# Sums of squares and two-element copies taken off GpSimd, and another beginning, in a two-layer hybrid decoder

## The chip, the cores and the metric

The kernel runs on one core of one Trainium2 chip. The metric is the device time of one execution in microseconds, as a median over several executions. The engines are named as the profile names them: PE is TensorE, PEld its weight load, DVE is VectorE, ACT is ScalarE, POOL is GpSimd, SP is SyncE, which issues the DMAs here.

## The reference

Two decoder layers run over x (256 positions, width 1024), all in float32. A vector c conditions every norm through a scale, a shift and a gate per feature:

```python
def rmsnorm(x, g):
    y = xf * lax.rsqrt(jnp.mean(xf * xf, axis=-1, keepdims=True) + RMS_EPS)
    return (y * g).astype(x.dtype)
def modulate(h, shift, scale):
    return h * (1 + scale[:, None, :]) + shift[:, None, :]

cs = jax.nn.silu(c)
mod = cs @ mod_w[l] + mod_b[l]                   # six vectors of 1024: sh_m, sc_m, g_m, sh_f, sc_f, g_f
h = modulate(rmsnorm(x, norm_mix[l]), sh_m, sc_m)
mix = rglru_mixer(...) if l == 0 else moba_mixer(...)
x = x + g_m[:, None, :] * mix
h = modulate(rmsnorm(x, norm_ffn[l]), sh_f, sc_f)
x = x + g_f[:, None, :] * swiglu(h, w_gate, w_up, w_down)
```

Before layer 1, x is normed once more for a shared key/value projection with its own shift and scale. The output is a last rmsnorm of x. The mixer of layer 0 is a gated linear recurrence with input and output projections; that of layer 1 is causal attention with 8 heads on 4 key/value heads. The feed-forward width is 2816.

## The kernel before, in words

**Layout.** Features lie on the partitions, positions on the free axis: x is eight tiles of 128x256, one for each group k of 128 features. A norm therefore sums over partitions. `sumsq` (lines 521 to 552) does it: ACT squares the eight tiles (L529), the squares are added up to fewer tiles (L538), and a product with a 128x128 matrix of ones (L543, "ones product" below, two PE instructions in float32) leaves the sum on every partition. ACT takes the root (L546), DVE the reciprocal (L551). The adds of the first norm, n0, run on DVE; those of the three later ones, f0, n2 and f1, run on POOL, six each, after which two tiles are left (`"sqpe": 1`) and two ones products follow.

**Products.** A float32 weight is split into a high part (ACT, L438) and a low part (DVE, L439), and one product is three fast matmuls (`mm3`, L386 to L388): high by high, high weight by low operand, low weight by high operand. A few products run in plain float32 instead (L448, L675), two PE instructions each.

**Borders.** In front of the products that follow a norm, the kernel does not wait for the norm. `unnorm` (lines 584 to 601) multiplies x by its scale alone, and the reciprocal root is applied to the product's result. The shift travels along as two more columns of the same operand: the tiles are 128x258. These columns are written by copies of two elements a partition on POOL, for the plain operand (L588) and for the high and low operand (L595). The names: `f_u` is the operand and `f_g` the product at the start of each feed-forward block (f0 in layer 0, plain, f1 in layer 1, split), `f_p` the products behind it; `kv_u` and `kp` are operand and product of the key projection (border n2); `f_d` is the down product of the feed-forward, `ao` the output product of the attention, `wo` that of the recurrence. The residuals that make the new x are on L609. L599 makes the low operand on DVE, L597 the high one on ACT.

**Scales and shifts.** A column of a modulation vector comes from a 512 KB block of weights in a slot of the pool `mraw` (three slots), which DVE multiplies by csb, the row silu(c) on all partitions, and sums up (L461); `_m` names are such vectors. Others go over PE.

**Start.** SP loads the row c (4 KB) into one partition of an `mraw` slot, then x, the small vectors and the first blocks. PE spreads the row with two ones products (L421), ACT takes Silu from PSUM (L423). Then the first norm, and for each k a column of scale and shift, the normed tile (L556), its high and low part (L562, L566, L567) and the input projection `xb` and `yb` (L675 and split).

**What sets the order.** A planner, `Plan` (lines 93 to 265), records every operation with a modelled cost, its buffers and a rank, which is its place in the program plus an offset from a table `PRIO` (by engine and name), and lists the operations per engine; each engine then runs its list in that order, and waits where an operand is missing. `KN` holds further offsets. The planner decides on every engine, SP's list of DMAs included.

## Time and profile before

| | |
|---|---|
| three runs | 622.88, 622.90, 624.37 us (median 622.90) |
| the profiled execution | 623.06 us |
| its span in the trace | 621.2 us |
| mean granted TensorE clock | 0.991 |
| TensorE busy | 593.1 us, 95% of the span, 4688 instructions |
| VectorE busy | 471.9 us, 76% |
| ScalarE busy | 338.1 us, 54% |
| GpSimd busy | 34.9 us, 6%, 68 instructions |
| moved by DMA | 162.95 MB, 262 GB/s in the mean |

The profiled execution took 623.06 us, of which 621.2 lie in the span of the trace; 1.9 us are outside it. In the order of time the stages are: the start and the input projection (to 52 us), the recurrence (52 to 107), its output product (to 135), border f0 and the first feed-forward (135 to 331), border n2 with the key projection (331 to 349), attention (349 to 419), border f1 and the second feed-forward (419 to 613), and a last norm. In the timeline a row is start, duration, engine, line, operation and tiles, count; a bracket gives the idle time before it and what released it. A matmul row lasts longer than the step to the next one, since they are pipelined.

### The profile page before, as it was taken

What the parts mean: (1) busy time and instruction counts of PE and PEld (TensorE: products, weight loads), DVE (VectorE), ACT (ScalarE), POOL (GpSimd) and SP (SyncE); (2) the same over time, 40 slices, a digit from 0 to 9 for tenths busy, and PEclk for the clock granted to TensorE, in tenths of its full rate; (3) what the DMA queues carried; (4) which work ended last, traced back from release to release, by engine and by line L of the source; (5) the groups of instructions that cost most, each with busy time, mean ns of one, the idle gap of its engine ahead of it and who ended that gap; (6) DMA issues with size and microseconds to landing.
All of it is one profiled execution on the core that took longest, in us unless ns stands there. A gap on an engine that the chain in (4) does not pass through costs nothing.

```text
span 621.2 us, 11500 instructions
## 1 busy us (share of the span) xinstructions
PE 593.1 (95%) x4688; PEld 569.8 (92%) x4688; DVE 471.9 (76%) x718; ACT 338.1 (54%) x485; POOL 34.9 (6%) x68
## 2 busy tenths in 40 slices
PE   3999999988999999999997999998999999999996
PEld 1899878987999999999996999997999999999996
DVE  6998888887988898998755799997997555545542
ACT  5537998537654344342445988766555434333322
POOL 0000000032000000001006000016000000000000
PEclk9999999999999999999998999997999999999999
DMA  8896897687988899898888257885696553445501
GB/s 297 335 356 241 326 390 324 244 316 293 413 314 313 326 332 329 331 342 345 325 314 286 70 203 306 301 323 190 213 333 234 181 179 141 140 143 187 185 1 69
DMA packets 33363, 162.95 MB, mean 262 GB/s; under 512 B 3700, under 2 KB 4893, under 8 KB 23966
## 3 DMA queue, kind: packets, MB, share of 16 engines
q1 hardware_dynamic: 33310, 162.21, 70.5%
q8 instruction: 37, 0.61, 0.4%
q14 instruction: 16, 0.13, 0.1%
...
## 4 chain that ended last, share of the span: by engine, by line
PE 80%; ACT 6%; DVE 4%; DMA 4%; POOL 2%; issue 2%; SPq 0%; DVEq 0%; POOLq 0%; ACTq 0%
PE ps_f_p L388 12%; PE ps_f_p L386 12%; PE ps_f_p L387 12%; PE ps_f_d L388 6%; PE ps_f_d L386 6%; PE ps_f_d L387 6%; PE ps_xb L675 2%; PE ps_f_g L448 2%; PE ps_yb L386 1%; PE ps_yb L388 1%; PE ps_yb L387 1%; PE ps_qp L388 1%; PE ps_qp L386 1%; PE ps_qp L387 1%; DMA mraw_mr_sc_f_m__1482<-in_mod 1%
## 5 line engine op out<-in xcount | busy, mean ns | idle before, releaser
L386 PE MATMUL ps_f_p<-t_f_h,whi_f0b_h 128*128 128x256 f32 x320 | 89.8, 281 | 0.0
L388 PE MATMUL ps_f_p<-t_f_h,wlo_f1b_l 128*128 128x256 f32 x320 | 89.6, 280 | 0.0
L387 PE MATMUL ps_f_p<-t_f_l,whi_f0b_h 128*128 128x256 f32 x320 | 89.4, 279 | 0.0
L388 PE MATMUL ps_f_p<-t_f_h,wlo_f0b_l 128*128 128x256 f32 x320 | 89.3, 279 | 0.0
L386 PE MATMUL ps_f_p<-t_f_h,whi_f1b_h 128*128 128x256 f32 x320 | 89.3, 279 | 0.0
L387 PE MATMUL ps_f_p<-t_f_l,whi_f1b_h 128*128 128x256 f32 x320 | 89.3, 279 | 0.0
L439 DVE TENSOR_TENSOR wlo_f1b_l<-raw_f1b_r,whi_f1b_h 128x2048 fp32r<-128x2048 f32 x20 | 45.8, 2289 | 21.0 <-ACT whi_f1b_h L438 20.9
L387 PEld LDWEIGHTS ps_f_p<-t_f_l,whi_f1b_h 128*128 128x128 f32 x320 | 60.2, 188 | 0.0
L388 PEld LDWEIGHTS ps_f_p<-t_f_h,wlo_f0b_l 128*128 128x128 f32 x320 | 60.2, 188 | 0.0
L386 PEld LDWEIGHTS ps_f_p<-t_f_h,whi_f0b_h 128*128 128x128 f32 x320 | 60.1, 188 | 0.0
L388 PEld LDWEIGHTS ps_f_p<-t_f_h,wlo_f1b_l 128*128 128x128 f32 x320 | 60.1, 188 | 0.0
L387 PEld LDWEIGHTS ps_f_p<-t_f_l,whi_f0b_h 128*128 128x128 f32 x320 | 59.9, 187 | 0.1
L386 PEld LDWEIGHTS ps_f_p<-t_f_h,whi_f1b_h 128*128 128x128 f32 x320 | 59.8, 187 | 0.0
L438 ACT ACTIVATE whi_f1b_h<-raw_f1b_r 128x2048 fp32r<-128x2048 f32 x20 | 38.1, 1911 | 26.5 <-issue 19.1
L439 DVE TENSOR_TENSOR wlo_f0b_l<-raw_f0b_r,whi_f0b_h 128x2048 fp32r<-128x2048 f32 x20 | 45.7, 2289 | 8.3 <-ACT whi_f0b_h L438 8.3
L438 ACT ACTIVATE whi_f0b_h<-raw_f0b_r 128x2048 fp32r<-128x2048 f32 x20 | 38.1, 1910 | 21.7 <-issue 18.5
L386 PE MATMUL ps_f_d<-t_f_ah,whi_f0c_h 128*128 128x256 f32 x176 | 49.4, 281 | 0.0
L388 PE MATMUL ps_f_d<-t_f_ah,wlo_f1c_l 128*128 128x256 f32 x176 | 49.3, 280 | 0.0
L388 PE MATMUL ps_f_d<-t_f_ah,wlo_f0c_l 128*128 128x256 f32 x176 | 49.1, 279 | 0.0
L386 PE MATMUL ps_f_d<-t_f_ah,whi_f1c_h 128*128 128x256 f32 x176 | 49.1, 279 | 0.0
L387 PE MATMUL ps_f_d<-t_f_al,whi_f1c_h 128*128 128x256 f32 x176 | 49.1, 279 | 0.0
L387 PE MATMUL ps_f_d<-t_f_al,whi_f0c_h 128*128 128x256 f32 x176 | 49.1, 279 | 0.0
...
## 6 DMA issues: line engine op xcount, KB each, us to landing
...
```

The costliest lines, as they stand in the source:

```text
L386: nc.tensor.matmul(o, h_, a_, start=start, stop=False, skip_group_check=skip)
L387: nc.tensor.matmul(o, h_, b_, start=False, stop=False, skip_group_check=skip)
L388: nc.tensor.matmul(o, l_, a_, start=False, stop=stop, skip_group_check=skip)
L438: act(n - o, lambda: nc.scalar.activation(hi.ap[:, o:n], raw.ap[:, o:n], AF.Copy), (raw,), (hi,))
L439: tt(n - o, lambda: nc.vector.tensor_sub(lo.ap[:, o:n], raw.ap[:, o:n], hi.f[:, o:n]), (raw, hi), (lo,))
L448: pe(n * 0.0016875 + 0.002, lambda: nc.tensor.matmul(ps.ap[:, c:c + n], lo.ap[:, o:o + w], xh.ap[:, xo:xo + n], start=start, stop=stop, sk ...
L675: pe(0.432, lambda k=k, m=m, c=c, ps=ps, wr=wr, f=f: nc.tensor.matmul(ps.ap[:, c:c + S], wr.ap[:, m * P:(m + 1) * P], f.ap[:, :S], start=( ...
```

## The change

1. **Another beginning.** The row c is no longer loaded into one partition. One DMA writes it to all 128 partitions of csb at once (512 KB written from a 4 KB row); it is fifth in SP's list, behind the four of x. One ACT Silu over 128x1024 follows in place. The two products on L421, the two Silus on L423 and the use of an `mraw` slot are gone.
2. **First norm.** The seven DVE adds of n0 become eight ones products: every square goes to PE.
3. **Norms at the borders.** For f0, n2 and f1 the six POOL adds become three DVE adds (of the first four squares), and five ones products instead of two (`"sqpe": 4`).
4. **Two-element copies.** Those of the high and of the plain operand go to ACT, those of the low operand to DVE: 8 on ACT in f0, 8 on ACT and 8 on DVE in n2 and in f1.
5. **The table of offsets** `PRIO` is another one on all engines, so the order moves everywhere, and POOL keeps 15 instructions.

```diff
-    "shat": 0, "gmat": 1, "win": 600, "tol": 3.6321997149340305e-16, "nn": 5, "nyh": 1, "sqpe": 1, "gnat": 5,
+    "shat": 0, "gmat": 1, "win": 600, "tol": 3.6321997149340305e-16, "nn": 5, "nyh": 1, "sqpe": 4, "gnat": 5,
...
     "PE": {
-        "cps": -707, "xb": 191, "ga": -492, "sh_f_ps": -94, "sh_f_pt": 1070, "wo": 33, "g_m_ps": 4, "g_m_pt": -155,
+        "n_st": 2072, "xb": -905, "yb": 4848, "ga": 540, "sh_f_ps": 1082, "sh_f_pt": -11, "wo": 288, "g_m_ps": -779,
...
-        crow = pl.buf("mraw", "crow")
-        load(crow, 8, lambda: crow.ap[0:1, :], t["c_row"])
+        pl.op("SP", 0.6, lambda: nc.sync.dma_start(csb.ap, t["c_row"].to_broadcast([P, D])), (), (csb,), lat=1.0)
...
-        silu = []
-        for i in range(2):
-            cps = PS(f"cps{i}")
-            c = slice(i * 512, (i + 1) * 512)
-            pe(0.86, lambda cps=cps, c=c: nc.tensor.matmul(cps.ap, ones.ap[0:1, :], crow.ap[0:1, c], start=True,
-                                                           stop=True), (ones, crow), (cps,))
-            silu.append(act(512, lambda cps=cps, c=c: nc.scalar.activation(csb.ap[:, c], cps.ap, AF.Silu), (cps,),
-                            ((csb, i),), AF.Silu))
+        silu = [act(D, lambda: nc.scalar.activation(csb.ap, csb.ap, AF.Silu), (csb,), (csb,), AF.Silu)]
...
-        def sumsq(xs, name, on_dve=False, prev=(), then=None):
+        def sumsq(xs, name, on_dve=False, on_pe=False, prev=(), then=None):
...
-                if acc is None:
+                if acc is None or on_pe:
                     acc = sq
                     parts.append(acc)
-                elif on_dve or k < KC - KN["sqpe"]:
+                elif (on_dve and name == "n0") or k < KC - KN["sqpe"]:
...
-                gp(2, 0.003, lambda: nc.gpsimd.tensor_copy(f.ap[:, S:], sh.ap[:, k:k + 1].to_broadcast([P, 2])), (sh,),
-                   ((f, 1),))
+                act(2, lambda: nc.scalar.activation(f.ap[:, S:], sh.ap[:, k:k + 1].to_broadcast([P, 2]), AF.Copy), (sh,),
+                    ((f, 1),))
...
-            for d, s_ in ((hi, shc[0]), (lo, shc[1])):
-                gp(2, 0.003, lambda d=d, s_=s_: nc.gpsimd.tensor_copy(d.r[:, S:], s_.r[:, k:k + 1].to_broadcast([P, 2])),
-                   (s_,), ((d, 1),))
+            act(2, lambda: nc.scalar.activation(hi.r[:, S:], shc[0].r[:, k:k + 1].to_broadcast([P, 2]), AF.Copy),
+                (shc[0],), ((hi, 1),))
+            tt(2, lambda: nc.vector.tensor_copy(lo.r[:, S:], shc[1].r[:, k:k + 1].to_broadcast([P, 2])), (shc[1],),
+               ((lo, 1),))
...
-        rstd0 = sumsq(x0, "n0", on_dve=True)
+        rstd0 = sumsq(x0, "n0", on_pe=True)
...
-            rstd = sumsq(xs, name, prev=(gelus, exps)[l], then=AF.Silu)
+            rstd = sumsq(xs, name, True, prev=(gelus, exps)[l], then=AF.Silu)
...
-        rstd2 = sumsq(x2, "n2", prev=silus[0], then=AF.Exp)
+        rstd2 = sumsq(x2, "n2", True, prev=silus[0], then=AF.Exp)
```

The lines of the changed kernel are six or seven lower than those of the kernel before: its splits are on L431 and L432, its square adds on L531, its residuals on L603, its low operands on L593 and its two-element copies on L587 (ACT) and L589 (DVE).

**Border n2 on DVE.** In the order of before, from the split of the value weights to the first low operands (`t_f0x` are the new x tiles, `ps_f_d` the down product, `t_kv_u_l` the low operand of the key product):

```order
L439 TENSOR_TENSOR wlo_wv_l<-raw_wv_r,whi_wv_h 128x2048
L609 SCALAR_TENSOR_TENSOR t_f0x_3748<-ps_f_d_3656,g_f_m,t_x_7_1573 128x256
L599 SCALAR_TENSOR_TENSOR t_kv_u_l<-t_f0x_3241,sc_kv_m,t_kv_u_h 128x256
L439 TENSOR_TENSOR wlo_wv_l<-raw_wv_r,whi_wv_h 128x2048
L599 SCALAR_TENSOR_TENSOR t_kv_u_l<-t_f0x_3319,sc_kv_m,t_kv_u_h 128x256
L599 SCALAR_TENSOR_TENSOR t_kv_u_l<-t_f0x_3416,sc_kv_m,t_kv_u_h 128x256
L599 SCALAR_TENSOR_TENSOR t_kv_u_l<-t_f0x_3494,sc_kv_m,t_kv_u_h 128x256
```

And in the changed kernel:

```order
L432 TENSOR_TENSOR wlo_wv_l<-raw_wv_r,whi_wv_h 128x2048
L593 SCALAR_TENSOR_TENSOR t_kv_u_l<-t_f0x_3229,sc_kv_m,t_kv_u_h 128x256
L593 SCALAR_TENSOR_TENSOR t_kv_u_l<-t_f0x_3313,sc_kv_m,t_kv_u_h 128x256
L603 SCALAR_TENSOR_TENSOR t_f0x_3759<-ps_f_d_3649,g_f_m,t_x_7_1574 128x256
L531 TENSOR_TENSOR t_n_sq_3761<-t_n_sq_3761,t_n_sq_3763 128x256
L531 TENSOR_TENSOR t_n_sq_3761<-t_n_sq_3761,t_n_sq_3765 128x256
L531 TENSOR_TENSOR t_n_sq_3761<-t_n_sq_3761,t_n_sq_3767 128x256
L432 TENSOR_TENSOR wlo_wv_l<-raw_wv_r,whi_wv_h 128x2048
L589 COPY t_kv_u_l<-kv_sl 128x2
L593 SCALAR_TENSOR_TENSOR t_kv_u_l<-t_f0x_3392,sc_kv_m,t_kv_u_h 128x256
```

The three square adds come onto DVE's list between the last residual and the second split of the value weights, and each low operand from the fourth on has a two-element copy ahead of it. The low operands of k = 1 and 2 now stand ahead of the last residual, with their copies earlier in the list.

**Border f1 on DVE.** In the order of before, from the shift vector to the third low operand (`ps_ao` is the attention's output product, `t_x` the new x, `wlo_f1a` the low part of the weights of `f_g`):

```order
L512 TENSOR_TENSOR sh_f_m<-sh_f_m,vec 128x8
L599 SCALAR_TENSOR_TENSOR t_f_u_l<-t_x_0_4798,sc_f_m,t_f_u_h 128x256
L609 SCALAR_TENSOR_TENSOR t_x_4_4839<-ps_ao_4572,g_m_m,t_f0x_3494 128x256
L609 SCALAR_TENSOR_TENSOR t_x_5_4851<-ps_ao_4572,g_m_m,t_f0x_3579 128x256
L581 TENSOR_TENSOR f_sl<-sh_f_m,f_sh 128x8
L439 TENSOR_TENSOR wlo_f1a_l<-raw_f1a_r,whi_f1a_h 128x2048
L599 SCALAR_TENSOR_TENSOR t_f_u_l<-t_x_1_4803,sc_f_m,t_f_u_h 128x256
L609 SCALAR_TENSOR_TENSOR t_x_6_4891<-ps_ao_4597,g_m_m,t_f0x_3668 128x256
L609 SCALAR_TENSOR_TENSOR t_x_7_4896<-ps_ao_4597,g_m_m,t_f0x_3748 128x256
L439 TENSOR_TENSOR wlo_f1b_l<-raw_f1b_r,whi_f1b_h 128x2048
L599 SCALAR_TENSOR_TENSOR t_f_u_l<-t_x_2_4815,sc_f_m,t_f_u_h 128x256
```

And in the changed kernel:

```order
L505 TENSOR_TENSOR sh_f_m<-sh_f_m,vec 128x8
L531 TENSOR_TENSOR t_f_sq_4804<-t_f_sq_4804,t_f_sq_4816 128x256
L603 SCALAR_TENSOR_TENSOR t_x_4_4832<-ps_ao_4559,g_m_m,t_f0x_3490 128x256
L531 TENSOR_TENSOR t_f_sq_4804<-t_f_sq_4804,t_f_sq_4823 128x256
L574 TENSOR_TENSOR f_sl<-sh_f_m,f_sh 128x8
L603 SCALAR_TENSOR_TENSOR t_x_5_4850<-ps_ao_4559,g_m_m,t_f0x_3581 128x256
L531 TENSOR_TENSOR t_f_sq_4804<-t_f_sq_4804,t_f_sq_4830 128x256
L603 SCALAR_TENSOR_TENSOR t_x_6_4859<-ps_ao_4576,g_m_m,t_f0x_3661 128x256
L589 COPY t_f_u_l<-f_sl 128x2
L593 SCALAR_TENSOR_TENSOR t_f_u_l<-t_x_0_4792,sc_f_m,t_f_u_h 128x256
L589 COPY t_f_u_l<-f_sl 128x2
L593 SCALAR_TENSOR_TENSOR t_f_u_l<-t_x_1_4799,sc_f_m,t_f_u_h 128x256
```

The split of `wlo_f1a` that stood ahead of the second low operand now stands behind it (it follows the residual of k = 7), and the three adds are interleaved with the residuals of k = 4 to 6.

**The start on DVE.** In the order of before, from the last adds of the first norm to the first normed tile (`mraw_mr_sc` and `mraw_mr_sh` are the blocks of the first scale and shift column):

```order
L641 TENSOR_SCALAR sp_m<-sp_neg 128x10
L538 TENSOR_TENSOR t_n_sq_218<-t_n_sq_218,t_n_sq_244 128x256
L461 SCALAR_TENSOR_TENSOR mraw_mr_sc__236,sc_138<-mraw_mr_sc__236,csb 128x1024
L661 SCALAR_TENSOR_TENSOR sc_138<-sc_138,b_137,vec 128x1
L461 SCALAR_TENSOR_TENSOR mraw_mr_sh__250,sh_139<-mraw_mr_sh__250,csb 128x1024
L551 RECIPROCAL t_n_rstd<-t_n_rstd 128x256
L664 TENSOR_TENSOR sh_139<-sh_139,vec 128x1
L556 TENSOR_TENSOR t_n_0_276<-t_x_0_210,t_n_rstd 128x256
```

And in the changed kernel:

```order
L618 TENSOR_SCALAR sp_neg<-vec 128x10
L635 TENSOR_SCALAR sp_m<-sp_neg 128x10
L619 TENSOR_TENSOR sp_ab<-sp_neg,vec 128x10
L454 SCALAR_TENSOR_TENSOR mraw_mr_sc__236,sc_138<-mraw_mr_sc__236,csb 128x1024
L544 RECIPROCAL t_n_rstd<-t_n_rstd 128x256
L655 SCALAR_TENSOR_TENSOR sc_138<-sc_138,b_137,vec 128x1
L454 SCALAR_TENSOR_TENSOR mraw_mr_sh__247,sh_139<-mraw_mr_sh__247,csb 128x1024
L549 TENSOR_TENSOR t_n_0_269<-t_x_0_208,t_n_rstd 128x256
```

The seven adds are gone from DVE's list, and the reciprocal stands behind the first block instead of behind the second. On PE's list the two products that spread the row are gone, eight ones products stand first, and the products `yb` of the first k follow behind `xb` instead of between.

## Rows read from the trace of the kernel before

**Rows 1.** The page, part 1: busy time, share of the span and instructions of each engine.

```profile
PE 593.1 (95%) x4688; PEld 569.8 (92%) x4688; DVE 471.9 (76%) x718; ACT 338.1 (54%) x485; POOL 34.9 (6%) x68
```

**Rows 2.** Waits of TensorE: line, what for; total us, times, longest us.

```profile
PE ps_xb L675 <- ACT t_h L562: 4.1, 1, 4.1
...
PE ps_kp L387 <- POOL t_kv_u_l L595: 4.0, 1, 4.0
...
PE ps_n_st L543 <- DVE t_n_sq L538: 3.4, 1, 3.4
...
PE ps_f_g L387 <- POOL t_f_u_l L595: 3.3, 2, 2.7
...
PE ps_cps L421 <- DMA mraw_crow<-in_c_row: 2.3, 1, 2.3
```

**Rows 3.** Windows: length, PE, PEld, DVE, ACT, POOL busy (count), clock, DMA share, GB/s.

```profile
20.00:30.00 10.00, 9.36 (x64) 8.75 (x65) 9.46 (x23) 6.95 (x11) 0.00 (x0) 1.00 0.97 379
...
140.00:150.00 10.00, 8.03 (x37) 6.70 (x36) 5.61 (x8) 5.76 (x10) 3.22 (x7) 1.00 0.67 266
...
330.00:340.00 10.00, 6.03 (x36) 5.44 (x35) 5.53 (x6) 3.33 (x6) 8.01 (x14) 0.86 0.92 308
...
420.00:430.00 10.00, 7.59 (x33) 6.87 (x34) 6.19 (x8) 4.16 (x10) 8.83 (x17) 0.66 0.73 266
...
430.00:440.00 10.00, 10.00 (x86) 10.00 (x85) 9.96 (x17) 9.35 (x15) 0.53 (x3) 1.00 0.33 119
```

**Rows 4.** Timeline of the n2 border: start us, us, instruction, [wait before <-releaser].

```profile
328.42 7.77 POOL L538 TENSOR_TENSOR t_n_sq<-t_n_sq,t_n_sq 128x256 f32<-128x256 f32 x5 [43.66 <-ACT t_n_sq L529]
...
330.86 0.28 PE L386 MATMUL ps_kp<-t_kv_u_h,whi_wk_h 128*128 128x258 f32 x1
...
336.57 0.39 PE L387 MATMUL ps_kp<-t_kv_u_l,whi_wk_h 128*128 128x258 f32 x1 [3.98 <-POOL t_kv_u_l L595]
...
349.08 0.28 PE L386 MATMUL ps_qp<-t_hq_h,whi_wq_h 128*128 128x256 f32 x1
...
331.81 1.07 DVE L599 SCALAR_TENSOR_TENSOR t_kv_u_l<-t_f0x,sc_kv_m,t_kv_u_h 128x256 fp32r<-128x256 f32 x1 [0.26 <-POOL t_n_sq L538]
...
333.25 2.37 DVE L439 TENSOR_TENSOR wlo_wv_l<-raw_wv_r,whi_wv_h 128x2048 fp32r<-128x2048 f32 x1 [0.37 <-ACT whi_wv_h L438]
```

**Rows 5.** Timeline of the f1 border.

```profile
418.83 0.28 PE L386 MATMUL ps_f_g<-t_f_u_h,whi_f1a_h 128*128 128x258 f32 x1
...
437.92 0.28 PE L386 MATMUL ps_f_p<-t_f_h,whi_f1b_h 128*128 128x256 f32 x1
...
415.71 1.65 DVE L609 SCALAR_TENSOR_TENSOR t_x<-ps_ao,g_m_m,t_f0x 128x256 f32<-128x256 f32 x4
...
417.28 0.15 DVE L512 TENSOR_TENSOR sh_f_m<-sh_f_m,vec 128x8 f32<-128x8 f32 x1
...
418.61 2.28 DVE L439 TENSOR_TENSOR wlo_f1a_l<-raw_f1a_r,whi_f1a_h 128x2048 fp32r<-128x2048 f32 x1
...
417.56 0.19 ACT L580 ACTIVATE f_sh<-sh_f_m 128x8 fp32r<-128x8 f32 x1
```

**Rows 6.** Timeline of the f0 border.

```profile
133.85 1.70 DVE L461 SCALAR_TENSOR_TENSOR mraw_mr_sc_f_m__1482<-mraw_mr_sc_f_m__1482,csb 128x1024 f32<-128x1024 f32 x1 [0.72 <-DMA mraw_mr_sc_f_m__1482<-in_mod]
...
137.45 3.31 PE L448 MATMUL ps_f_g<-t_f_u_f,raw_f0a_r 128*128 128x258 f32 x14 [1.80 <-POOL t_f_u_f L588]
...
142.73 0.70 PE L543 MATMUL ps_f_st<-t_f_sq,ones 128*128 128x256 f32 x2 [1.97 <-POOL t_f_sq L538]
...
154.39 0.47 PE L386 MATMUL ps_f_p<-t_f_h,whi_f0b_h 128*128 128x256 f32 x1
```

**Rows 7.** Timeline of the start.

```profile
9.31 1.21 DVE L461 SCALAR_TENSOR_TENSOR mraw_mr_sc__236<-mraw_mr_sc__236,csb 128x1024 f32<-128x1024 f32 x1
...
14.74 4.63 PE L675 MATMUL ps_xb<-t_h,raw_wix 128*128 128x256 f32 x10 [4.08 <-ACT t_h L562]
...
20.64 0.39 PE L388 MATMUL ps_yb<-t_h_h,wlo_wix_l 128*128 128x256 f32 x1 [0.84 <-DVE wlo_wix_l L439]
```

47 lines of the change are left out of this document (24 added, 23 removed).

## The prediction

> **What bounds the kernel now.** I read the page's busy times first. TensorE is busy 593.1 of 621.2 us, 95% [rows 1]: no other engine is near, and at most 28 us can be had without taking work from it. So I asked next where TensorE is not working. Its waits name two places: the start, with 4.1, 3.4 and 2.3 us, and three borders, where GpSimd is named as the releaser: 4.0 us at n2 and 3.3 at f1 [rows 2], 1.80 and 1.97 at f0 [rows 6]. The windows then show a second loss that no wait shows: in 330 to 340 the granted clock is 0.86 and in 420 to 430 it is 0.66, after the two longest border waits, so matmuls run for a time at the lower of the two levels (1.2 instead of 2.4 GHz). It is 1.00 in 140 to 150, where a wait of 1.97 us lies [rows 3, 6]. So a wait of 2 us here costs itself, one of 2.7 to 4 costs itself and a stretch at half speed. For work at full clock I use the window 430 to 440: 86 matmuls in 10.00 us, 0.12 us each [rows 3].
>
> **GpSimd is not the only one late.** The name in a wait is the last releaser. At n2 DVE's split of `wlo_wv` runs from 333.25 for 2.37 us [rows 4], and before's order puts the low operand that PE needs behind it: it could not be there before 336.0 (0.41 behind the split's end), against the 336.57 at which PE went on. At f1 the split at 418.61 (2.28 us) [rows 5] stands ahead of the second low operand in the same way. Taking the copies off GpSimd alone would return half a microsecond. The new order lets those low operands overtake the splits; the gain needs both.
>
> **Border n2.** From the first `kp` matmul (330.86) to the first `qp` (349.08) are 18.22 us [rows 4]. The work in them is 96 matmuls at 0.12, or 11.5, and two ones products. For a ones product I take f0: from 137.45 to 154.39 less the wait of 1.97 are 14.97 us for 68 float32 instructions [rows 6], 0.22 each, two a product: 0.44. So 12.4 us of work and 5.8 of loss, 3.98 of it the wait, the rest half clock. With the change PE has three ones products more (1.3), and twelve of the 96 matmuls move ahead among the down products, which shifts them and costs nothing. If PE does not wait, the border takes 11.5 + 5 x 0.44 = 13.7, a gain of **4.5**. What could be late instead is DVE. A residual, an add or a low operand costs it about 0.41 (four residuals in 1.65 [rows 5]). Its list: last residual about 331.6, three adds to 333.2, the split to 335.6 if the weight's high part comes when it did (333.25 [rows 4]), a copy and the fourth low operand to 336.1. PE meanwhile has k = 1 and 2 (24 matmuls, 2.9), five ones products (2.2) and a small product of 0.7, from about 331.5: to 337.3. DVE is 1.2 us ahead, and after that each k costs PE 1.44 and DVE 0.6.
>
> **Border f1.** From 418.83 to 437.92 are 19.09 us [rows 5]: 12.4 of work, 6.7 of loss. With five ones products and no wait it would be 13.7, a gain of 5.4. Here DVE is nearer: `ao` ends at 418.83, but four residuals end only at 417.4 [rows 5], and three adds, three more residuals (each 0.41) and short ones (estimated at 0.1 to 0.2 from the short row of 0.15) follow before the first low operand, so the ones product on the adds waits to about 419.4 (0.6), and the third low operand, behind the last residual and a split of 2.28, comes about 0.3 to 0.8 late. These waits are under 1 us each, so I leave the clock full. Gain 5.4 - 1.1 = **4.3**; bounds 2.5 and 5.4.
>
> **Border f0.** The waits of 1.80 and 1.97 [rows 6] go, three ones products (1.3) come. But the first `f_g` needs the last column of the scale, whose block DVE has at 133.85 by its transfer [rows 6]; the new order multiplies it before the first residual. Then 1.3 for the column, four residuals at 0.41 and the short steps: the first operand is ready about 137.5, no earlier than the 137.45 of before. From there 64 + 10 instructions at 0.22 are 16.3: end 153.8 against 154.39. Gain **0.6**, bounds 2.5 (1.80 + 1.97 - 1.3) and -1.
>
> **Tiny copies.** 24 on ACT (0.19, a row of eight columns) and 16 on DVE (0.15) [rows 5] are 4.6 and 2.4 us in all, on engines busy 54% and 76% [rows 1]; at the borders they are in the sums above, elsewhere PE's 100% covers them. Without that cover, f0's eight would cost 1.5.
>
> **The shared access.** One low operand on DVE took 1.07 us while GpSimd added, where four residuals of the same size took 1.65 without it; five adds took 7.77 [rows 4, 5]. My sums use the undisturbed 0.41. The Trainium skill (SBUF — State Buffer, the rules on contention) says that a DVE instruction with two SBUF inputs and a GpSimd one that reads SBUF exclude each other for a whole instruction; the rows agree. Were the 1.07 DVE's own price, f1 would lose 0.66 on each of three low operands, 2.0 us, and the sum would end at 615.
>
> **Start.** The two spreading products and their wait of 2.3 go, but the first `xb` at 14.74 [rows 7] is what counts. Before, DVE's multiply for the first column began at 9.31, right behind its seven adds [rows 7]. Now it waits for csb: 0.52 MB behind x, at 379 GB/s [rows 3] 1.4 us, less a DMA issue of 0.4 ahead of x, then a Silu on 1024 columns (about 1 us, estimated from a low operand's 0.41 for 256 with its fixed part). I take the first column at 9.8 and, with reciprocal and second block behind it, `xb` 0.9 later. PE's wait of 0.84 at 20.64 [rows 7] goes, since the split of the first weights moves up and `yb` moves back; I count 0.5 more, an estimate, for the `yb` matmuls around that wait, which now come when their operands have long been there. Everything behind is bound by PE and DMA (0.97 busy [rows 3]). Net gain 0.84 + 0.5 - 0.9, **0.4**, bounds 2.5 (ten float32 matmuls in 4.63 us [rows 7], which would take 2.2 at full clock) and -1.5 (csb's transfer paid whole).
>
> **The rest.** The recurrence waits little and the attention is reordered with all operands early; I take 0, bounds 1.5 either way. Both feed-forward bodies stay PE at 100%.
>
> **Sum.** 4.5 + 4.3 + 0.6 + 0.4 = 9.8. From the profiled execution's 623.06 (0.16 above the median of 622.90) that is 613.3; against the median 613.1. I give **613.2**, and 610 to 616 as this case's own range. About 0.3%, 1.9 us, is what a measurement here can tell from no change.
>
> **Rivals.**
> - *DVE becomes the bound at the borders.* For: it is busy 9.96 of 10 us right after f1 [rows 3], and takes adds and copies. Against: it also loses GpSimd's disturbance. If the low operands trail the splits again, PE waits 2 us at n2 and at f1 and the clock falls: half of the 8.8 goes, 613.2 + 4.4 = 617.6. Chance 0.17.
> - *More goes than I count.* The first products meet a full clock (2.2) and the small waits of the recurrence and of f0 close (2): 609. Chance 0.12.
> - *The waits are renamed.* The weights, not the operands, end last: DMA is 0.92 busy in 330 to 340 [rows 3], and the value weights' high part came at 333.25 [rows 4]. Then both borders keep their length: 622. Against: the `kp` weights themselves were long there. Chance 0.06.
> - *The broadcast is slow, and the kernel slower.* All sixteen early columns need csb, the first `xb` too. If the one 4 KB row is read again and again through one of the 16 DMA engines, 0.52 MB go at 379/0.97/16 = 24 GB/s [rows 3]: 22 us instead of 1.4, and with every column 20.6 us later 634. Lateness of 9.8 us, the gain of the rest, is the point from which it decides. Against: 128 destination rows can be shared out. The Trainium skill (DMA: Bandwidth & Descriptors, the table of best practices) says that the outermost dimension sets how many engines share a transfer, and that a broadcast of fewer than 16 copies outermost confines it; here it is 128, so by it this does not happen, and no row of before shows it. Chance 0.05.
>
> **How the numbers follow.** My forecast has 0.60. Faster: forecast, DVE rival and the better case, 0.89. The same: most of the renamed waits, 0.05. Slower: the broadcast and a remainder, 0.06. For 8 in 10 the range takes in the DVE rival and the near part of the better case: 609.0 to 618.0.
>
> **What would show it.** Right: the waits on GpSimd are gone, clock 1.00 at both late borders, `kp` to `qp` about 13.7 us, `f_g` to `f_p` of f1 14.8, first `xb` near 15.6. Wrong: waits named DVE or ACT of 2 us or more there with the clock below 0.9, or a first `xb` past 17.

## The result, and the profile of the changed kernel

The change makes the kernel faster by a little over one per cent. Four runs took 614.68, 615.15, 617.90 and 627.78 us, median 616.52, against 623.18 before; the ratio is 0.988 with an interval of 0.9841 to 0.9918. The same kernel was run twice more among the experiments below, beside before on other occasions: 617.69 (ratio 0.9891) and 618.06 us (0.9887). So the gain is 6 to 7 us where 9.7 were forecast. The ratios, here and below, leave out executions that lie over 1.5% above the fastest of their kernel (here the 627.78) and the medians do not, so that a kernel with a wide spread (a_pool, h2) looks better by its ratio. The profiled execution took 615.15 us with a span of 613.3, which is 7.9 under the span of before; it is one of the better executions, which the reader should keep in mind.

The busy times of the page, to set beside [rows 1]:

```profile
PE 592.4 (97%) x4716; PEld 571.9 (93%) x4716; DVE 468.7 (76%) x736; ACT 341.0 (56%) x508; POOL 1.2 (0%) x10
```

TensorE has 28 instructions more and as much work as before, in a shorter span. GpSimd's 34.9 us are 1.2, in 10 instructions. ACT is 2.9 us busier with its copies; DVE took nine adds and 16 copies over, gave up the seven adds of n0, and is 3.2 us less busy.

The waits of TensorE (line, what for; total us, times, longest us), beside [rows 2]:

```profile
PE ps_xb L669 <- ACT t_h L555: 6.8, 2, 5.8
PE ps_n_st L536 <- ACT t_n_sq L522: 3.9, 1, 3.9
PE ps_sh_f_ps L469 <- ACT whi_wiy_h L431: 1.9, 1, 1.9
PE ps_f_st L536 <- DVE t_f_sq L531: 1.4, 2, 1.1
PE ps_kp L388 <- DVE t_kv_u_l L593: 1.0, 1, 1.0
```

No wait names GpSimd. The 4.0 us at n2 are 1.0, now for a low operand of DVE. The 3.3 at f1 are one wait of 1.1 for the adds (the rest of that row lies at f0). What stands on top now is the start, with 5.8 us in front of the first `xb`. The windows, columns as in [rows 3]:

```profile
10.00:20.00 10.00, 4.17 (x13) 3.35 (x13) 9.23 (x19) 4.92 (x8) 0.05 (x1) 0.66 0.98 372
140.00:150.00 10.00, 9.79 (x45) 8.25 (x45) 7.90 (x8) 7.88 (x12) 0.00 (x0) 1.00 0.45 170
330.00:340.00 10.00, 8.99 (x61) 7.60 (x61) 9.79 (x18) 9.19 (x24) 0.00 (x0) 1.00 0.93 347
420.00:430.00 10.00, 10.00 (x86) 10.00 (x85) 9.64 (x18) 8.29 (x18) 0.00 (x0) 1.00 0.48 154
```

The clock is 1.00 behind both late borders, where it was 0.86 and 0.66. The 0.66 in 10 to 20 is not a new loss: the first ten `xb` products took 4.63 us in before [rows 7] and take 4.03 here, 0.46 and 0.40 each against 0.22 at f0. So both kernels begin at the slow pace; the trace of before holds no record of the clock ahead of 19.7 us, and its 1.00 there stands for nothing recorded.

**Where the time went.** I cut both traces at TensorE's own milestones. A piece runs from the first or last matmul of one product to that of the next; in us:

| piece | before | after | difference |
|---|---|---|---|
| start to the first `ga` | 55.57 | 56.16 | +0.59 |
| first `ga` to the first `wo` (recurrence) | 51.35 | 51.91 | +0.56 |
| `wo` | 28.23 | 28.15 | -0.08 |
| last `wo` to the first `f_p` (f0) | 19.24 | 17.14 | -2.10 |
| first `f_p` to the last `f_d` | 176.36 | 177.29 | +0.93 |
| last `f_d` to the first `qp` or `vp` (n2) | 18.33 | 14.58 | -3.75 |
| to the last `ao` (attention) | 69.63 | 69.43 | -0.20 |
| to the last `f_d` (f1 and the second feed-forward) | 194.34 | 190.50 | -3.84 |

Two of these are shifted against each other by the order. Twelve `kp` matmuls (1.42) moved up among the down products, and a small product of 0.74 moved the other way; so n2 gained 3.07 and the first feed-forward lost 0.25. The differences add up to the 7.89 by which the last `f_d` comes earlier.

Border n2 in the timeline, PE first and then DVE and ACT, to set beside [rows 4]:

```profile
330.77 0.28 PE L387 MATMUL ps_kp<-t_kv_u_h,whi_wk_h 128*128 128x258 f32 x1
332.05 0.39 PE L388 MATMUL ps_kp<-t_kv_u_l,whi_wk_h 128*128 128x258 f32 x1 [1.01 <-DVE t_kv_u_l L593]
...
334.91 2.32 PE L536 MATMUL ps_n_st<-t_n_sq,ones 128*128 128x256 f32 x10
337.16 0.81 PE L928 MATMUL ps_rp<-t_oneh,relt 33*8 33x384 f32 x2
...
329.31 2.29 DVE L432 TENSOR_TENSOR wlo_wv_l<-raw_wv_r,whi_wv_h 128x2048 fp32r<-128x2048 f32 x1 [0.45 <-ACT whi_wv_h L431]
331.52 0.87 DVE L593 SCALAR_TENSOR_TENSOR t_kv_u_l<-t_f0x,sc_kv_m,t_kv_u_h 128x256 fp32r<-128x256 f32 x2
...
327.35 1.92 ACT L431 ACTIVATE whi_wv_h<-raw_wv_r 128x2048 fp32r<-128x2048 f32 x1 [0.82 <-DMA raw_wv_r<-in_wv]
```

The 1.01 us are the old fault in small. The low operand for k = 1 stands behind a split of the value weights (329.31), that split waited for ACT's high part, and ACT for the weights' transfer (0.82). A low operand alone is now about 0.4 (two in 0.87), where one took 1.07 beside GpSimd. Border f1, beside [rows 5]:

```profile
416.08 1.10 PE L536 MATMUL ps_f_st<-t_f_sq,ones 128*128 128x256 f32 x4 [1.14 <-DVE t_f_sq L531]
416.83 0.47 PE L387 MATMUL ps_f_g<-t_f_u_h,whi_f1a_h 128*128 128x258 f32 x1
...
428.76 0.28 PE L387 MATMUL ps_f_p<-t_f_h,whi_f1b_h 128*128 128x256 f32 x1
...
413.98 0.42 DVE L531 TENSOR_TENSOR t_f_sq<-t_f_sq,t_f_sq 128x256 f32<-128x256 f32 x1
...
416.25 0.16 DVE L589 CAST t_f_u_l<-f_sl 128x2 fp32r<-128x2 f32 x1
416.31 0.48 DVE L593 SCALAR_TENSOR_TENSOR t_f_u_l<-t_x,sc_f_m,t_f_u_h 128x256 fp32r<-128x256 f32 x1
```

The start, beside [rows 7]:

```profile
8.43 1.06 ACT L417 ACTIVATE csb<-csb 128x1024 f32<-128x1024 f32 x1 [1.18 <-DMA csb<-in_c_row]
...
10.77 1.22 DVE L454 SCALAR_TENSOR_TENSOR mraw_mr_sc__236<-mraw_mr_sc__236,csb 128x1024 f32<-128x1024 f32 x1 [0.99 <-DMA mraw_mr_sc__236<-in_mod]
...
13.63 1.22 DVE L454 SCALAR_TENSOR_TENSOR mraw_mr_sh__247<-mraw_mr_sh__247,csb 128x1024 f32<-128x1024 f32 x1
...
15.95 4.03 PE L669 MATMUL ps_xb<-t_h,raw_wix 128*128 128x256 f32 x10 [5.83 <-ACT t_h L555]
...
37.33 2.43 PE L669 MATMUL ps_xb<-t_h,raw_wix 128*128 128x256 f32 x10 [1.00 <-ACT t_h L555]
...
35.84 0.95 ACT L431 ACTIVATE whi_wix_h<-raw_wix 128x896 fp32r<-128x896 f32 x1 [5.13 <-DMA raw_wix<-in_win_x]
```

csb is there at 9.49. What DVE waits for at 10.77 is the first block of weights, which lies behind csb's 512 KB in the queue. At 37.33 TensorE waits once more, which it did not in before: the operand `t_h` stands on ACT behind a split (35.84) that waited for its weights' transfer.

### The profile page after: what moved, and what is told of

It is laid out like the page before. It is cut to its first block, busy times and chain, and to the rows that moved or that the text cites. A ratio compares the mean times of both kernels' runs of the same rounds, so it can differ in the third digit from the quotient of the medians.

```text
span 613.3 us, 11433 instructions
## 1 busy us (share of the span) xinstructions
PE 592.4 (97%) x4716; PEld 571.9 (93%) x4716; DVE 468.7 (76%) x736; ACT 341.0 (56%) x508; POOL 1.2 (0%) x10
## 4 chain that ended last, share of the span: by engine, by line
PE 56%; DMA 20%; DVE 15%; ACT 4%; issue 4%; SPq 1%; DVEq 0%; ACTq 0%
PE ps_f_p L387 9%; PE ps_f_p L388 9%; PE ps_f_p L389 9%; PE ps_f_d L387 3%; PE ps_f_d L389 3%; PE ps_f_d L388 3%; DVE wlo_f0c_l L432 2%; PE ps_ga L441 2%; DVE wlo_f0b_l L432 2%; PE ps_xb L669 1%; DMA mraw_mr_sh_m_m__3257<-in_mod 1%; PE ps_qp L388 1%; DMA raw_wix<-in_win_x 1%; PE ps_qp L387 1%; PE ps_qp L389 1%
## 5 line engine op out<-in xcount | busy, mean ns | idle before, releaser
L432 DVE TENSOR_TENSOR wlo_f1b_l<-raw_f1b_r,whi_f1b_h 128x2048 fp32r<-128x2048 f32 x20 | 45.6, 2290 | 20.3 <-ACT whi_f1b_h L431 20.3
L431 ACT ACTIVATE whi_f1b_h<-raw_f1b_r 128x2048 fp32r<-128x2048 f32 x20 | 38.3, 1913 | 27.6 <-issue 19.1
L431 ACT ACTIVATE whi_f0b_h<-raw_f0b_r 128x2048 fp32r<-128x2048 f32 x20 | 38.2, 1910 | 21.8 <-issue 19.1
L432 DVE TENSOR_TENSOR wlo_f0b_l<-raw_f0b_r,whi_f0b_h 128x2048 fp32r<-128x2048 f32 x20 | 45.8, 2288 | 5.4 <-ACT whi_f0b_h L431 5.3
```

Source lines behind the costliest of these rows:

```text
L431: act(n - o, lambda: nc.scalar.activation(hi.ap[:, o:n], raw.ap[:, o:n], AF.Copy), (raw,), (hi,))
L432: tt(n - o, lambda: nc.vector.tensor_sub(lo.ap[:, o:n], raw.ap[:, o:n], hi.f[:, o:n]), (raw, hi), (lo,))
```

## The experiments

The order of the operations decides much here, and the planner gives another order to every edit. So all kernels but the two repetitions replay a written list of operations and buffers in the planner's place; with the lists of before and of after that gives the engines' own sequences back. Times are medians, ratios are to before in the same set of runs.

| run | median us (lowest to highest, runs) | ratio, interval | profiled us |
|---|---|---|---|
| after_again | 617.69 (615.02 to 620.64, 6) | 0.9891, 0.9850 to 0.9933 | 619.05 |
| after_2 | 618.06 (614.64 to 620.83, 6) | 0.9887, 0.9845 to 0.9929 | 618.94 |
| b_nopool | 618.82 (616.86 to 620.84, 8) | 0.9913, 0.9884 to 0.9942 | 618.57 |
| a_pool | 622.93 (615.46 to 628.72, 12) | 0.9928, 0.9888 to 0.9968 | 623.29 |
| a_copies | 616.87 (1) | one run, no ratio | 616.87 |
| a_oldstart | 620.96 (616.65 to 624.71, 12) | 0.9948, 0.9917 to 0.9980 | 621.86 |
| h1 | 622.69 (618.12 to 625.28, 12) | 0.9972, 0.9940 to 1.0004 | 619.26 |
| h1_new | 620.72 (617.28 to 624.20, 12) | 0.9951, 0.9924 to 0.9977 | 617.28 |
| h2 | 619.95 (611.11 to 627.10, 12) | 0.9898, 0.9859 to 0.9937 | 619.01 |
| hf1 | 618.84 (615.49 to 622.06, 11) | 0.9904, 0.9872 to 0.9936 | 621.11 |
| hf1_new | 619.34 (615.03 to 627.11, 12) | 0.9915, 0.9884 to 0.9945 | 624.16 |
| hf1_fd | 616.81 (612.21 to 621.70, 6) | 0.9858, 0.9824 to 0.9893 | 617.03 |

And the pieces of the profiled executions, cut as above (us):

| run | first `xb` at | to `ga` | recurrence | f0 | first f-f | n2 | f1 and second f-f |
|---|---|---|---|---|---|---|---|
| after_again | 16.36 | 57.96 | 53.47 | 17.58 | 177.23 | 14.05 | 190.84 |
| after_2 | 15.91 | 57.01 | 52.21 | 16.01 | 181.54 | 13.34 | 191.02 |
| b_nopool | 14.75 | 55.25 | 51.60 | 18.11 | 176.49 | 16.32 | 192.95 |
| a_pool | 16.71 | 59.31 | 53.30 | 17.53 | 177.52 | 14.58 | 193.05 |
| a_copies | 16.03 | 60.55 | 51.48 | 16.00 | 177.02 | 13.35 | 190.93 |
| a_oldstart | 15.05 | 57.38 | 55.56 | 16.06 | 181.19 | 13.35 | 190.76 |
| h1 | 15.39 | 57.89 | 52.41 | 18.11 | 178.34 | 13.67 | 190.93 |
| h1_new | 15.82 | 57.43 | 52.00 | 18.11 | 177.93 | 14.43 | 189.75 |
| h2 | 15.42 | 58.16 | 52.00 | 18.10 | 177.72 | 13.54 | 191.56 |
| hf1 | 14.69 | 55.67 | 51.25 | 18.50 | 183.29 | 13.59 | 190.49 |
| hf1_new | 16.79 | 57.77 | 51.42 | 18.50 | 181.69 | 14.17 | 192.97 |
| hf1_fd | 15.06 | 55.72 | 52.29 | 18.51 | 177.24 | 15.48 | 189.92 |

With the new order behind n2 (all but b_nopool), 0.68 us belong to n2 that stand in the first feed-forward.

**after_again: the changed kernel once more, with a profile.**

> The changed kernel as it is. Its four runs lay between 614.7 and 627.8 us, those of before within 1.5 us. If the wide ones were disturbances of the chip, five rounds here give 615 to 616 with a spread like that of before. If the new order has a weak place that some executions hit (a transfer that comes just in time), again one run in three or more lies 2 us or more above the fastest, and the clock shows it, below 0.99.

Measured: the borders are what they were (14.05, 190.84, and 17.58 at f0), yet this execution took 3.9 us longer than the first. The difference lies at the start (57.96 against 56.16) and in the recurrence (53.47 against 51.91). In the latter a wait of 1.9 became 2.2 and names the transfer of `raw_sh_f_r` itself, and the clock in 80 to 90 is 0.83, where it was 1.00. The borders' gain is there again; what varies is in front of them. The sign that I had named for a weak place in the new order, a wide spread, does not serve: after's six executions lie between 615.02 and 620.64, and the 25 of before beside them between 618.70 and 628.33.

**b_nopool: nothing on GpSimd, with before's order and beginning.**

Each norm keeps its six adds and two ones products; the copies move as in the change (those of f0's plain operand, not shown here, to ACT too).

```diff
-            rstd = sumsq(xs, name, prev=(gelus, exps)[l], then=AF.Silu)
+            rstd = sumsq(xs, name, True, prev=(gelus, exps)[l], then=AF.Silu)
...
-            for d, s_ in ((hi, shc[0]), (lo, shc[1])):
-                gp(2, 0.003, lambda d=d, s_=s_: nc.gpsimd.tensor_copy(d.r[:, S:], s_.r[:, k:k + 1].to_broadcast([P, 2])),
...
+            act(2, lambda: nc.scalar.activation(hi.r[:, S:], shc[0].r[:, k:k + 1].to_broadcast([P, 2]), AF.Copy),
...
+            tt(2, lambda: nc.vector.tensor_copy(lo.r[:, S:], shc[1].r[:, k:k + 1].to_broadcast([P, 2])), (shc[1],),
```

> Before, in before's own order, with GpSimd's six adds at each border and its two-element copies on DVE and ACT in the places where the order had them. My theory (both GpSimd and the order were in the way): the wait of 1.97 us at f0 goes, n2 gains about 2 since ACT no longer waits for GpSimd's adds, f1 only 0.5 because the split of wlo_f1a still stands ahead of the second low operand: 618 to 620 us, with the f1 wait still there and the clock still lowered behind it. Rival (GpSimd was the whole cause): 613 to 615. Rival (the order was all): 622 to 623.

Measured: ratio 0.9913 and 618.82 us, as expected; f1 gained more than the 0.5 that I had given it. The waits that are left at the borders:

```profile
PE ps_f_g L669 <- DVE t_f_u_l L878: 2.8, 1, 2.8
...
PE ps_f_g L730 <- ACT t_f_u_f L870: 2.1, 1, 2.1
...
PE ps_kp L669 <- DVE t_kv_u_l L878: 1.9, 1, 1.9
```

and the windows at n2 and f1:

```profile
330.00:340.00 10.00, 8.05 (x50) 7.49 (x49) 8.93 (x19) 6.83 (x16) 0.00 (x0) 0.83 0.91 312
...
420.00:430.00 10.00, 9.50 (x65) 9.19 (x64) 9.62 (x20) 7.14 (x18) 0.00 (x0) 0.85 0.54 206
```

This shows that GpSimd was not the only one late. With nothing on it, the wait at f1 is as long as before (2.8 against 2.7) and the one at n2 half as long (1.9 against 4.0), both now named DVE, and the clock still falls. Against before, n2 gains 2.0, f1 1.4 and f0 1.1. The rest of what after's first profile has at n2 and f1, about 1.1 (16.32 against 14.58 + 0.68) and 2.4, is the new order and the ones products, which this run does not separate. In the medians the two kernels can't be told apart: after's profiles reach the first `wo` 1.2 to 4.6 us later (108.07 to 111.43 against 106.85), which is about what they have more at the borders.

**a_pool: after, with adds and copies back on GpSimd.**

```diff
-            rstd = sumsq(xs, name, True, prev=(gelus, exps)[l], then=AF.Silu)
+            rstd = sumsq(xs, name, prev=(gelus, exps)[l], then=AF.Silu)
...
-            act(2, lambda: nc.scalar.activation(hi.r[:, S:], shc[0].r[:, k:k + 1].to_broadcast([P, 2]), AF.Copy),
...
+                gp(2, 0.003, lambda d=d, s_=s_: nc.gpsimd.tensor_copy(d.r[:, S:], s_.r[:, k:k + 1].to_broadcast([P, 2])),
```

> The changed kernel in its own order, with the three adds of each border and the two-element copies back on GpSimd, nothing else touched. My theory: three adds of 0.7 to 1.5 us fit beside DVE's work at n2 (0 to 1 us lost), but at f1 they end some 2 us later than DVE's did, PE waits on the ones products or on the copies behind them and the clock falls: 617 to 619 us. Rival (the order was all): 615. Rival (GpSimd was the whole cause): 621 to 623.

Measured: f1 with its feed-forward is 193.05, 2.0 to 2.6 longer than in the three executions of after; n2 is 14.58 as in the first of them, although DVE's adds went to GpSimd there too. At f1 the adds are late:

```profile
419.95 0.74 POOL L812 TENSOR_TENSOR t_f_sq<-t_f_sq,t_f_sq 128x256 f32<-128x256 f32 x1 [75.00 <-ACT t_f_sq L803]
420.63 0.19 POOL L869 CAST t_f_u_h<-f_sh 128x2 fp32r<-128x2 f32 x1
420.77 0.73 POOL L812 TENSOR_TENSOR t_f_sq<-t_f_sq,t_f_sq 128x256 f32<-128x256 f32 x1
...
421.59 0.91 POOL L812 TENSOR_TENSOR t_f_sq<-t_f_sq,t_f_sq 128x256 f32<-128x256 f32 x1
...
422.55 1.13 PE L817 MATMUL ps_f_st<-t_f_sq,ones 128*128 128x256 f32 x4 [2.00 <-POOL t_f_sq L812]
...
336.20 1.83 DVE L873 SCALAR_TENSOR_TENSOR t_kv_u_l<-t_f0x,sc_kv_m,t_kv_u_h 128x256 fp32r<-128x256 f32 x2
```

An add is 0.73 to 0.91 on GpSimd here, 0.42 on DVE, and TensorE waits 2.0 us for the third. Behind that wait the clock is 0.83 in 420 to 430. With the new order, adds and copies on GpSimd cost f1 2.0 to 2.6 us. At n2 the cost is small: the two low operands (336.20) take 1.83 us beside GpSimd's adds in place of 0.87, so about half a microsecond of the 0.99 that TensorE waits at `kp` is GpSimd's. The time of the whole kernel does not decide between the rivals: the twelve executions lie between 615.46 and 628.72 us, the median of 622.93 lies with "GpSimd was the whole cause", the ratio of 0.9928 with my own theory, and the profile lost 4.5 us in front of the first `wo`.

**a_copies: after, with only the two-element copies back on GpSimd** (the second part of the diff of a_pool).

> The changed kernel with the two-element copies alone back on GpSimd, the adds on DVE. One look, read by stage. My theory (the adds cost GpSimd time, the copies alone cost nothing): n2 from the last down product to the first product behind it within 0.4 us of the changed kernel's 14.1 to 14.6, and from the last ao product to the last down product 190.5 to 191. Rival (the copies were what PE waited for, as the wait list of before says): 192 or more in the second, as with both back on GpSimd (193.05).

Measured: n2 13.35 (below the 13.7 to 15.0 that I had allowed), f1 190.93, 616.87 us. The copies on GpSimd cost nothing that this profile shows at these borders, so in this order it is the adds that count in the move. The copies alone were not moved in before's order.

**a_oldstart: after, with before's beginning** (the row in one partition, two spreading products, seven DVE adds).

```diff
-        pl.op("SP", 0.6, lambda: nc.sync.dma_start(csb.ap, t["c_row"].to_broadcast([P, D])), (), (csb,), lat=1.0)
+        crow = pl.buf("mraw", "crow")
+        load(crow, 8, lambda: crow.ap[0:1, :], t["c_row"])
-        rstd0 = sumsq(x0, "n0", on_pe=True)
+        rstd0 = sumsq(x0, "n0", on_dve=True)
```

> The changed kernel in its own order, with the start of before: the row spread by two products on PE into PSUM and two Silus, the first norm's adds on DVE, one ones product. My theory (the broadcast's half megabyte holds back the blocks behind it): the first xb comes 1 us or more earlier, near 14.5 us, and 0.5 to 1.2 us of it are left at the end: 614 to 614.7. Rival (the start is bound further on, by transfers and PE): the first xb is earlier but the end is the same, 615.2. Rival (the seven adds on DVE hold the first column as they did before): 615.5 or more.

Measured: a miss. The first `xb` came at 15.05, where I had said 14.5, there was no gain at the front (57.38 and 55.56), and the median is above after's. The run does not answer its question. My list gave the first block of modulation weights the slot of the row c, which had to come free first; so SP issued that block, and the input weights behind it, some 2.5 us late (the latter at 7.04 in place of 4.59). It shows something else: 181.19 in the first feed-forward, to which hf1 comes back.

**h1, h1_new and h2: before's order up to the recurrence's end, after's order behind.** h1 has before's beginning, h1_new the new one; h2 is h1 with DVE's low operands of k = 1 and 2 ahead of the first value split at n2, and the first low operand of f1 ahead of the second add (with ACT's split and PE's first twelve `f_g` products moved to match).

> A mixture: everything up to the recurrence's output product in before's order and with before's beginning (row spread on PE, the first norm's adds on DVE), everything behind it in the changed kernel's order and on its engines. My theory (the new order of the start and the recurrence costs 1 to 6 us, since its transfers come later, and hides part of what the borders give): the output product of the recurrence starts near 107 us again instead of 108 to 113, the borders keep their lengths, and the time is 2 to 4 us below that of the changed kernel on the same chip. Rival (this chip's transfers were slow in those runs, whatever the order): the output product starts at 110 or later here too, and the time is that of the changed kernel, ratio to before 0.989.

> As the mixture before it, but with the new beginning (broadcast by transfer, eight ones products) in before's order of the start. If the new beginning itself is what costs, the first xb comes 1.2 to 1.6 us later than in the mixture and the recurrence's output product starts later by 0.5 to 1.6 us. If only the order of the start costs, that product starts within 0.3 us of the mixture's.

> The mixture with two small moves at the borders: at n2 the operands of k = 1 and 2 ahead of the first split of the value weights on ACT and DVE; at f1 the first low operand ahead of the second and third square add, and the first twelve products of f_g ahead of the ones products. My theory (what is left of the waits there is DVE's order, not its load): the waits of 0.5 to 1.0 us at n2 and 1.1 to 1.5 us at f1 go, 1.5 to 2.5 us in all below the mixture. Rival (DVE and ACT are full there): the waits move to later operands and the time stays within 0.5 us of the mixture's.

Measured: h1 and h2 have the same flaw at the start as a_oldstart; in h1 the first `wo` came at 110.3, later than the 108.1 of after's first profile, so what I expected of it missed. h1_new has no row in a slot and so not the flaw; its first `wo` came at 109.4, 0.9 earlier than h1's, and against h1 it says nothing on the beginning. h2's two moves brought no time: n2 13.54 against 13.67, f1 191.56 against 190.93. At f1 the wait for the adds, 1.58 in h1, became two of 0.3 in front of `f_g` and two of 0.2 and 0.35 behind it, which is the rival that I had named. At n2 h1's own profile has no wait that the move could have taken away. One execution of h2 took 611.11 us, the shortest of all runs, but its median is 619.95.

**hf1 and hf1_new: the same with the slots put right.** hf1 is before up to the last `wo` (beginning, order and slots), and after from there; hf1_new differs from hf1 in the beginning alone.

> The mixture again (beginning and order of before up to the recurrence's output product, order and engines of the changed kernel behind it), now with the buffers of the early part in before's slots: in the mixture before it the first weight block had been given the slot of the row c and waited for it. My theory (before's early part is the faster one by 1 us or more, and loses that when its first blocks come late): output product of the recurrence at 106.5 to 107.5 us in the profile, f0, n2 and f1 as in the changed kernel, 612 to 615 us and below the changed kernel of the same call. Rival (the early part differs from run to run by the transfers' pace, not by the order): the output product starts at 109 or later, and the time is that of the changed kernel within 1 us.

> The same mixture with before's slots, but with the new beginning: broadcast by transfer, eight ones products, no row in a slot. If the new beginning costs by itself (half a megabyte ahead of the first blocks), the first xb comes 1 us or more later than in the mixture with the old one and the recurrence's output product 0.5 to 1.5 us later. If it is hidden by what bounds the stage behind it, that product starts within 0.3 us of the other's.

Measured: in hf1 the first `wo` comes at 106.92, as in before (55.57 + 51.35), and n2 and f1 are after's (13.59, 190.49). In hf1_new the first `xb` comes 2.1 us later (16.79 against 14.69) and the first `wo` 2.3 later (109.19). So with everything else alike, the new beginning cost over 2 us in these two profiles; the medians differ by 0.5 us in the same direction, which is less than their intervals can tell. The other profiles point the same way: the four that begin as before does, without the flaw (before, b_nopool, hf1, hf1_fd), reach `ga` at 55.25 to 55.72, the seven with the new beginning at 56.16 to 60.55, and two of these seven, h1_new and hf1_new, have before's order there. (At f1 hf1_new shows how thin the cover is: TensorE waited 2.0 us for DVE's adds, and the piece is 192.97.) But hf1 as a whole did not win (618.84, where I had said 612 to 615): f0 is 18.50, since the column's transfer did not come earlier with the rest, and it lost 6 to 7 us where no border is, at the end of the first feed-forward's up products. DVE and PE of hf1 there, with the window:

```profile
274.56 1.22 DVE L744 SCALAR_TENSOR_TENSOR mraw_mr_sh_m_m__3009<-mraw_mr_sh_m_m__3009,csb 128x1024 f32<-128x1024 f32 x1 [0.96 <-DMA mraw_mr_sh_m_m__3009<-in_mod]
275.71 0.08 DVE L744 DVE_READ_ACCUMULATOR mraw_mr_sh_m_m__3009<-mraw_mr_sh_m_m__3009,csb 128x1 f32 x1
275.71 0.69 DVE L1190 TENSOR_TENSOR t_f_f<-ps_f_p,t_f_s 128x512 f32<-128x512 f32 x1
...
277.11 0.58 PE L669 MATMUL ps_f_d<-t_f_ah,whi_f0c_h 128*128 128x256 f32 x1 [2.78 <-ACT t_f_ah L888]
...
270.00:280.00 10.00, 6.72 (x46) 6.22 (x46) 8.56 (x17) 5.65 (x8) 0.00 (x0) 0.83 0.89 340
```

The last elementwise product of the block, `t_f_f`, stands in DVE's new order behind a column that is multiplied when its weights arrive. The last up product had ended at about 267.3. In before such columns stood there too, but the one ahead of `t_f_f` waited for nothing.

**after_2: the changed kernel a third time, beside hf1.**

> The changed kernel once more, so that the two mixtures stand beside it on one chip. A ratio to before near 0.989 as in the first two comparisons, a first xb near 16 us, and the recurrence's output product between 108 and 112 us.

Measured: the same weak place in the changed kernel itself.

```profile
273.31 1.23 DVE L454 SCALAR_TENSOR_TENSOR mraw_mr_sh_m_m__3003<-mraw_mr_sh_m_m__3003,csb 128x1024 f32<-128x1024 f32 x1 [2.26 <-DMA mraw_mr_sh_m_m__3003<-in_mod]
...
275.87 0.38 PE L387 MATMUL ps_f_d<-t_f_ah,whi_f0c_h 128*128 128x256 f32 x1 [1.84 <-ACT t_f_ah L598]
```

The first feed-forward took 181.54 here and 177.29 in the first profile, where the same column waited 1.19 us in place of 2.26, and TensorE not at all. Here the borders were at their best (n2 13.34, f0 16.01), and the execution was no faster for it. The two belong together: TensorE reached n2 4.3 us later than in the first profile, and the first split of the value weights began only 2.4 later. In after's three profiles that split began 1.3, 1.9 and 3.2 us ahead of the last `f_d`, and TensorE waited 1.0, 0.5 and 0 us at `kp`.

**hf1_fd: hf1 with that one place reordered.** On DVE, ahead of the last split and the late column (names only; on ACT `t_f_ah` goes ahead of a split as well):

```diff
-wlo_f0c_l   sc_m_m   sh_m_m column   t_f_f   sh_m_m column   t_f_al
+sc_m_m   t_f_f   t_f_al   wlo_f0c_l   sh_m_m column   sh_m_m column
```

> hf1 with one piece of the order changed: at the end of the first up products the elementwise product t_f_f of the last pair, its high part on ACT and its low part on DVE go ahead of the last split of that place and of the columns that wait for a transfer. Theory (the loss at f_d is a matter of this order): TensorE's wait on t_f_ah, 2.8 us in hf1's profile, and the half clock behind it are gone; from the first f_p to the last f_d 177 to 178 us in place of 183.3; the profile 614 to 616 where hf1's was 621.1, the median 613 to 616, under the change's own 616.5 to 618. Rival (the transfers set the pace there, not the order): the wait goes to a later split or residual, this stretch stays above 181 us and the median within 617 to 620. A third possibility: the stretch falls but the median does not, because the loss at f_d is not in most executions.

Measured: the first feed-forward is 177.24 in place of 183.29, and the wait on `t_f_ah` is gone.

```profile
269.18 0.68 DVE L1190 TENSOR_TENSOR t_f_f<-ps_f_p,t_f_s 128x512 f32<-128x512 f32 x1
270.56 0.69 DVE L889 TENSOR_TENSOR t_f_al<-t_f_f,t_f_ah 128x512 fp32r<-128x512 f32 x1 [0.70 <-ACT t_f_ah L888]
...
272.79 1.21 DVE L744 SCALAR_TENSOR_TENSOR mraw_mr_sh_m_m__3009<-mraw_mr_sh_m_m__3009,csb 128x1024 f32<-128x1024 f32 x1
...
270.00:280.00 10.00, 10.00 (x87) 10.00 (x86) 6.80 (x9) 4.57 (x4) 0.00 (x0) 1.00 0.84 290
```

But this profile does not show the reordering at work, since the transfer that made hf1 wait was not late in it. The column that had stood ahead of `t_f_f` began at 272.79 without a wait, 4.2 us behind the end of the last up product (268.6); in hf1 it was 7.3 us. Over the eleven profiles that have after's order at this place, the column began 2.1 to 4.7 us behind in the seven in which TensorE did not wait for `t_f_ah`, and 6.2 to 7.3 in the four in which it did (after_2, a_oldstart, hf1, hf1_new). By hf1's own steps (1.15 us for the column, 1.40 from `t_f_f` to the next `f_d`, work for TensorE until 7.1 us behind the last up product) `t_f_ah` would have come at 275.3 in the old order here and TensorE run out of work at 275.7; these two times are estimates. So the cause is read from the rows and from the eleven profiles: the wait comes where this column is late, with `t_f_f` behind it. That the reordering cures it was not shown.

Of what I expected, the 177 to 178 us came; the profile (617.03) and the median missed the 616 by a little, and the third possibility, that most executions do not have this loss, fits four profiles in eleven. The ratio is 0.9858, the lowest of the set; with all six executions it is 0.988. The kernel is not shown to beat after: its interval overlaps after's, its median of 616.81 is after's 616.52 within the scatter, and 1.9 us of its profile went to n2, where the split began only 0.4 us ahead of the last `f_d` and a low operand was 1.8 late.

## Why the prediction was right, and by how much it was off

The time came out at 616.5, inside the wider range (609.0 to 618.0), just outside the narrower one (610 to 616) and 3.3 above the number given; the two repetitions lie at the wider range's edge. By the time alone the rival with DVE as the bound (617.6) fits better than the forecast. The traces decide against it: it wanted waits of 2 us at both late borders with the clock falling, and they are 1.0 and 1.1 us at a clock of 1.00. Direction and mechanism hold, and the sum was too large. Against the first profile, term by term:

- **What bounds the kernel.** Right. The waits of GpSimd and the half clock behind them were the loss, and both went: clock 1.00 at both late borders.
- **"GpSimd is not the only one late."** Right, with a correction. b_nopool has the waits renamed to DVE, 1.9 and 2.8 us, and a_pool is the other half, the new order with adds and copies still on GpSimd. Against before, each in one profile, n2 gains 2.0 us by the move alone, 3.1 by the new order with its ones products alone, and 3.1 by both (4.3 in after_2); f1 gains 1.4, 1.6 and 4.0. So "the gain needs both" holds at f1; at n2 the order does nearly all. The "half a microsecond" for the copies alone was not run in before's order; in after's they cost nothing (a_copies), and adds and copies together returned 2.0 and 1.4 in b_nopool.
- **n2, forecast 4.5, measured 3.1.** The step that failed is "DVE is 1.2 us ahead". I let the low operands overtake one split; the order puts another, of the value weights, ahead of the first two. It came late by its transfer, and TensorE waited 1.01. In after_2, with no wait at `kp`, n2 is 13.34, 1.24 shorter, and the term nearly met (4.3); but that is luck, since TensorE came to the border 4.3 us late there.
- **f1, forecast 4.3, measured 4.0** for the border: from the last `ao` 14.1 us and 1.07 for nine `f_g` matmuls that moved behind the first `f_p`, 15.2, against 19.2. The forecast wait for the adds was 0.6 and is 1.1; the one for the third low operand did not come.
- **f0, forecast 0.6, measured 2.1.** The work was right: 16.47 us from `f_g` to `f_p`, forecast 16.3. But I held the operand's time fixed (137.5) and missed that the last `wo` would come later, at 136.22 in place of 135.15, by the 1.1 us lost in front of it. The column came at 133.22, 0.6 earlier than before, so that most of the old wait went. So 1.1 of the 2.1 only gives back what was lost in front, and f0's surplus of 1.5 over the forecast covers in the sum what the start and the recurrence missed: luck again. In the three profiles of after this border is 16.0 to 17.6, as the column's transfer falls.
- **Start, forecast a gain of 0.4, measured a loss of 0.6** at the first `ga`, and of 1.4 and 2.4 in the other two profiles. csb came as forecast (9.49, I said 9.8 for the column behind it). Two steps failed. I charged csb's 1.4 us of transfer to csb alone, and not to what lies behind it in the queue: the first block of weights landed at 10.7, and the column began 1.0 later than forecast. The first `xb` came only 0.3 behind the forecast all the same (15.95 against 15.6). The larger part, 0.7, was missed behind it, where I had counted 1.34 us of gain and 0.62 came: the wait of 0.84 in front of `yb` went, but a new one of 1.00 stands at 37.33, for an operand behind a split of late weights. hf1 against hf1_new puts the price of this beginning at 2.3 us by the end of the recurrence, in one pair of profiles.
- **The rest, forecast 0 with 1.5 either way.** The recurrence lost 0.6 here and up to 2.1 (after_again), in front of `sh_f_ps`, whose weights come late: TensorE waits 1.9 to 3.7 us there in the profiles with the new order, and none to 1.7 in those with before's. "Both feed-forward bodies stay PE at 100%" failed in after_2: 4.2 us at `f_d`. I never looked at which operands DVE's new order puts behind a column that waits for a transfer.

The rivals: waits renamed, slow broadcast and DVE as the bound did not come true. The broadcast was not confined to one engine's 24 GB/s: issued at 2.59, it was used at 8.43, so its 0.52 MB moved at 90 GB/s or more, and the first `xb` came 1.2 us late, not 20. The Trainium skill (DMA: Bandwidth & Descriptors, Rules for kernel authors) says that an outermost dimension below 16 confines a transfer to that many engines; the time agrees that 128 copies were not confined to one. The Trainium skill (SBUF — State Buffer, Who interferes with whom) says that a DVE instruction with two SBUF inputs contends with a GpSimd instruction that reads SBUF. The traces agree: two low operands take 0.87 us in after and 1.83 beside GpSimd's adds in a_pool.

The gain that is missing, then, was not lost at the borders, which gave 9.2 us of the 9.4 forecast. It was given back in front of them and in the first feed-forward, at places where work that TensorE needs stands behind a transfer: the first columns and splits, `sh_f_ps`, and `t_f_f`, the last only with after's order. Different executions lose at different ones; after's lie between 614.6 and 620.8 us. The spread is not the new order's alone, since before's lie between 618.7 and 628.3 beside them. Why the transfers come a microsecond earlier or later from one execution to the next stays open.
